# Strassen groups of a decoder layer: eviction bank by bank, two patterns, and loads at other places

## The chip, the core and the metric

The kernel runs on one core of a Trainium2 chip. A core has a matrix engine (TensorE, PE in the profile, with its weight loads as PEld), a vector engine (VectorE, DVE), a scalar engine (ScalarE, ACT), GpSimd (POOL), and a queue that issues most transfers (SyncE, SP). Each engine works through its own queue in order. Products land in PSUM, a memory of eight banks of 128 × 512 float32; everything else works in SBUF. The metric is the device time of one execution in microseconds (us), as the median of several runs.

## The reference

One layer on 256 tokens of width 2048: a SwiGLU block (FFN 1), a mixing block (sliding-window attention beside a gated linear recurrence), a second SwiGLU block (FFN 2), a gated embedding, and a final norm.

```python
def swiglu(h, w_gate, w_up, w_down):
    return (jax.nn.silu(h @ w_gate) * (h @ w_up)) @ w_down
...
        h = rmsnorm(x, ffn1_norm[l])
        x = x + 0.5 * swiglu(h, ffn1_w_gate[l], ffn1_w_up[l], ffn1_w_down[l])

        h = rmsnorm(x, mix_norm[l])
        proj = h @ w_in[l]
...
        x = x + merged @ w_out[l]

        h = rmsnorm(x, ffn2_norm[l])
        x = x + 0.5 * swiglu(h, ffn2_w_gate[l], ffn2_w_up[l], ffn2_w_down[l])

        g = jax.nn.sigmoid(rmsnorm(x, ple_norm[l]) @ ple_w_gate[l])
        x = x + g * (p[l].astype(x.dtype) @ ple_w_proj[l])
    return rmsnorm(x, final_norm)
```

The gate and up weights of an FFN are 2048 × 5632, the down weights 5632 × 2048, all float32.

## The kernel before

**Numbers in two parts.** Products are made from float32 values that are split into a high and a low part: ScalarE copies a weight block to `whi` (L117), VectorE subtracts it to get `wlo` (L118), and three products (high × high, high × low, low × high) are summed in PSUM. A weight block is 128 × 1024 floats, 512 KB, and is called an item below. `Weights` (L32 to L133) keeps the items' order: `load` issues the transfer of an item on SyncE (L92, eight buffers `raw`), `prep` makes its two parts (five buffers each for `whi` and `wlo`), `next` hands it out, prepares four items ahead (`AHEAD`) and calls `pump`. `pump` counts: a function given to `later(n, fn)` is called at the n-th pump from then, so n is a place in the order of items.

**The order of instructions.** The kernel is written with a scheduler in front: it puts the instructions of each engine in an order when the program is built, by readiness in its own estimate of time and by priority, which is the order of writing unless `high_priority(offset)` moves it ahead by that many instructions. Loads and splits of items after the twelfth have `PRIO`, 3000 (L87, L102). `keep_in_program_order` pins a transfer behind what was written before it on its queue (L533). At run time each engine keeps that order and waits at the head of its queue for what is not ready.

**The FFN.** `ffn` (L443) goes through the 11 chunks of 512 hidden columns in five slices (`FF_SLICES`): the chunks of a slice, then a share of the down products, four output blocks `nb` of 512 columns each (L488). A chunk's result `e` is transposed and split into `act` tiles by `to_act` (`transpose_split`, L327); those of a slice are queued behind its last chunk, the first two at once, the others at later pumps (L483 to L487). Chunk 0 of FFN 1 is computed plainly, while the activations' scale is still being made. The other 21 chunks go through `strassen_group` (L381).

**A Strassen group** computes gate and up of one chunk, for two halves of 128 tokens. The inner dimension is cut into four quarters `q`. `PATTERN` (L138) gives each a kind. A quarter "S" makes seven products of sums (roles 0 to 6: P1, P2, Q3, Q6, Q7, Q5, P4), one bank each, six matmuls each; its weights are four items and sums of them (L108 to L112, three at role 3, one at role 6). A quarter "P" makes the products plainly, four items of twelve matmuls: gate into the banks P2 and P4, up into Q3 and PE_. With "SPSP" P1, Q6, Q7 and Q5 are complete after the third quarter and the other four after the last. The banks are combined by nine instructions, one copy on ScalarE (L418) and eight additions on VectorE (`tt`, L402): p1, v2 and three more after the third quarter, in the order of writing (L415 to L422), and four at the end (L435 to L440), with SiLU in between (`silu`, L468, handed in as `last_first`). Then `e` = up × SiLU(gate) (L473, in FFN 2 L475 with a scale). None of these has a raised priority. All eight PSUM banks are used by a group: four from `acc`, four from `misc`, and transposes and down products take theirs from the same two.

**The activations of a group** are made by `scaled_parts` (L345): x, scaled and transposed, is split for a quarter "P" (`ap`, L251) or summed and split for a quarter "S" (`af` L365 and L369, `as` L373 and L374). In FFN 1 this needs the whole of x for the norm: `load_x` (L544) loads the eight pieces at pumps 4 to 7 (L551) and sums their squares (L255); `r_first` makes the scale; `scaled_parts` of quarter q comes at pump 9 + q (L643).

**Constants of the mixing block** are made by `mix_constants` (L572) at pump 60 (L638), which is the last item of chunk 2, the last of FFN 1's first slice: small loads on SyncE (L574, `hlb` among them), two loads of masks, and 44 short instructions on VectorE (L578 to L636) with some on ScalarE.

**The pumps of FFN 1**: chunk 0 has 16 items, every group 22, a slice's down products 16 (the last slice's 24). So pumps 279 to 300 are chunk 10, and 301 to 324 the last down products.

Of the kernel before, what the change touches and what calls it, by code (L numbers as in the profile page):

```python
# [10 lines left out]
F32 = mybir.dt.float32  # L11
# [7 lines left out]
P = 128  # L19
# [115 lines left out]


FF_SLICES = (((0, 3), (0, 2)), ((3, 5), (2, 4)), ((5, 7), (4, 6)), ((7, 9), (6, 8)), ((9, 11), (8, 11)))
PATTERN = "SPSP"  # L138
MIX = (
    ("i", 0), ("fq", 0), ("fq", 1), ("og", 0), ("kv", 0), ("fq", 2),  # L140
    ("q", 0), ("fq", 3), ("q", 1), ("i", 1), ("og", 1),
# [4 lines left out]
def weight_order():  # L146
    order = []

    def add(name, *idx):
        order.append((name, tuple(idx)))  # L150

    def block(name, nb, kg1=8, kg0=0):
        for kg in range(kg0, kg1):
            add(name, kg, nb)

    def ffn(n):
        for (a, b), (da, db) in FF_SLICES:
            for c in range(a, b):
                g, u = f"ffn{n}_gate", f"ffn{n}_up"
                if n == 1 and c == 0:  # L160
                    block(g, c)
                    block(u, c)
                    continue
                for q, kind in enumerate(PATTERN):
                    if kind == "S":
                        order.extend(("S", (g, c), (u, c), q, role) for role in range(7))
                    else:
                        order.extend((v, (2 * q + k, c)) for k in range(2) for v in (g, u))
            for nb in range(4):
                block(f"ffn{n}_down", nb, 2 * db, 2 * da)  # L170

    ffn(1)
    for what, j in MIX:
        if what == "fq":
            for h in (2 * j, 2 * j + 1):
                for w in ("w_f", "w_q"):
# [20 lines left out]
def decoder_layer(ctx: ExitStack, tc: tile.TileContext, io, out):  # L197
# [144 lines left out]
                nc.tensor.transpose(pt[:, c, t * P:(t + 1) * P], srcs[t][:, i * P:(i + 1) * P], ident)  # L342
        return pt

    def scaled_parts(A, q, s, gain):  # L345


        xs = [etile(name="xs") for _ in range(2)]
        for t in range(2):
            nc.scalar.activation(xs[t], x[t][q], AF.Copy, scale=s[:, t:t + 1])  # L350
        if PATTERN[q] == "P":
            A[q] = [atile(name="ap") for _ in range(2)]
            for kp in range(2):
                pt = transposed(xs, kp, "tx")
                for c in range(2):
                    f = 4 * q + 2 * kp + c
                    split_scaled(A[q][kp][:, c], pt[:, c], gain[:, f:f + 1])
            return
        full = [atile([P, 4, 2, P], F32, name="af") for _ in range(2)]
        quarter = full[0].rearrange("p (k c) t n -> p k c t n", k=2)  # L360
        for kp in range(2):
            pt = transposed(xs, kp, "tx")
            for c in range(2):
                f = 4 * q + 2 * kp + c
                nc.scalar.activation(quarter[:, kp, c], pt[:, c].rearrange("p (t n) -> p t n", t=2), AF.Copy, scale=gain[:, f:f + 1])  # L365
        a11, a21, a12, a22 = (quarter[:, k, :, t] for k in range(2) for t in range(2))
        a5, a6, a7, a3 = (full[1][:, i] for i in range(4))
        for o, u, v in ((a5, a21, a22), (a6, a11, a5), (a7, a21, a11), (a3, a12, a6)):
            nc.vector.tensor_tensor(o, u, v, op=ALU.subtract)  # L369
        parts = []  # L370
        for i in range(2):
            hi, lo = (atile([P, 4, 2, P], name="as") for _ in range(2))
            nc.scalar.copy(hi, full[i])  # L373
            nc.vector.tensor_tensor(lo, full[i], hi.bitcast(F32), op=ALU.subtract)  # L374
            parts.append((hi, lo))
        (rh, rl), (ch, cl) = parts
        raw = lambda k, t: lambda c: (rh[:, 2 * k + c, t], rl[:, 2 * k + c, t])
        mix = lambda i: lambda c: (ch[:, i, c], cl[:, i, c])
        A[q] = (raw(0, 0), raw(1, 0), mix(3), mix(1), mix(2), mix(0), raw(1, 1))

    def strassen_group(first, second, A, last_first):  # L381


        banks = {}
# [8 lines left out]
        for i in range(7):  # L393
            bank(i)

        def mm(i, stat, mov):
            todo = 6 * PATTERN.count("S") * (i < 7) + 12 * PATTERN.count("P") * (i in (P2, Q3, P4, PE_))
            done[i] = done.get(i, 0) + 1
            nc.tensor.matmul(bank(i), stat, mov, start=done[i] == 1, stop=done[i] == todo)  # L399

        def tt(out, a, b, op):
            nc.vector.tensor_tensor(out, a, b, op=op)  # L402

        g, u = (atile([P, 2, 512], F32, name="ff") for _ in range(2))
        for q, kind in enumerate(PATTERN):
            if kind == "S":
                for role in range(7):
                    hi, lo = (v.rearrange("p (c n) -> p c n", c=2) for v in W.next(("S", first, second, q, role)))
# [3 lines left out]
                        mm(role, sl, hi[:, c])  # L412
                    for c in range(2):
                        mm(role, A[q][role](c)[0], lo[:, c])
                if q == PATTERN.rindex("S"):  # L415
                    tmp = atile([P, 2, 512], F32, name="st")
                    p1, v2 = tmp[:, 0], tmp[:, 1]
                    nc.scalar.copy(p1, banks[P1])  # L418
                    tt(v2, banks[Q6], p1, ALU.subtract)
                    tt(g[:, 1], banks[Q7], v2, ALU.add)  # L420
                    tt(u[:, 0], banks[Q5], v2, ALU.add)
                    tt(u[:, 1], banks[Q5], g[:, 1], ALU.add)  # L422
            else:
                for k in range(2):
                    for (name, nb), (b0, b1) in ((first, (P2, P4)), (second, (Q3, PE_))):
# [6 lines left out]
                        for c in range(2):  # L432
                            for t, b in enumerate((b0, b1)):
                                mm(b, A[q][k][:, c, 0, t * P:(t + 1) * P], lo[:, c])
        tt(g[:, 0], banks[P2], p1, ALU.add)  # L435
        last_first(g, 0)
        tt(g[:, 1], banks[P4], g[:, 1], ALU.subtract)
        last_first(g, 1)
        tt(u[:, 0], banks[Q3], u[:, 0], ALU.add)
        tt(u[:, 1], banks[PE_], u[:, 1], ALU.add)  # L440
        return g, u

    def ffn(n, A, hT, r_of, on_block):  # L443
# [8 lines left out]
        for (a, b), (da, db) in FF_SLICES:  # L452
            for c in range(a, b):
# [13 lines left out]
                def silu(g, t):  # L467
                    nc.scalar.activation(g[:, t], g[:, t], AF.Silu, scale=1.0 if n == 1 else r_of()[:, t:t + 1])  # L468

                e, u = strassen_group((gate, c), (up, c), A, silu)  # L470
                for t in range(2):
                    if n == 1:
                        nc.vector.tensor_tensor(e[:, t], u[:, t], e[:, t], op=ALU.mult)  # L473
                    else:
                        nc.vector.scalar_tensor_tensor(e[:, t], u[:, t], r_of()[:, t:t + 1], e[:, t], op0=ALU.mult, op1=ALU.mult)  # L475
                es[c] = e
            late = []
            for c in range(da, b):
# [69 lines left out]
    load_in_order(ident, io["ident"])  # L548
    for nb in range(4):
        for t in range(2):  # L550
            W.later(4 + nb, lambda t=t, nb=nb: load_x(t, nb))  # L551
    first = []

    def r_first():
# [14 lines left out]
    omlb = const.tile([P, 8], F32, name="omlb")  # L569
    cs = const.tile([P, 2, 2, 16], F32, name="cs")  # L570

    def mix_constants():  # L572
        for t_, n_ in ((cpT, "cpT"), (sink, "sink"), (hlb, "hlb"), (pos, "pos"), (freq, "freq")):
            load_in_order(t_, io[n_])  # L574
        nc.gpsimd.memset(neg, -3.0e38)
        wide = atile([P, 512], I32, name="wide")
        load_in_order(wide, io["masks"][:, 0:512])
        nc.vector.tensor_copy(lmask.rearrange("p a s -> p (a s)"), wide)  # L578
        wide = atile([P, P], I32, name="wide")
        load_in_order(wide, io["masks"][:, 512:640])  # L580
        nc.vector.tensor_copy(pmask, wide)


        lmx = const.tile([P, 8], F32, name="lmx")
# [50 lines left out]
            nc.scalar.activation(cs[:, t, 1, 0:8], ang[:, t], AF.Sin)  # L635
            nc.vector.tensor_copy(cs[:, t, :, 8:16], cs[:, t, :, 0:8])  # L636

    W.later(60, mix_constants)  # L638

    mhT, on_block, mrs = next_stage("mx", gains["mix"])  # L640
    A1 = {}
    for q in range(4):
        W.later(9 + q, lambda q=q: scaled_parts(A1, q, r_first(), gains["ffn1"]))  # L643
    ffn(1, A1, hT, r_first, on_block)
    hT = mhT

# [242 lines left out]
    def on_block(nb):  # L889

        for t in range(2):
            square_sum(ss2[:, t, nb:nb + 1], x[t][nb])
        if nb == 2:
            s3 = const.tile([P, 2], F32, name="s3")
            v3 = const.tile([P, 2], F32, name="v3")
            nc.vector.tensor_reduce(v3, ss2[:, :, 0:3], axis=AX.X, op=ALU.add)
            nc.vector.tensor_scalar(v3, v3, 1.0 / 1536, EPS, op0=ALU.mult, op1=ALU.add)
            nc.gpsimd.tensor_tensor(s3, v3, nhalf[:, 0:2], op=ALU.pow)
            nc.vector.tensor_tensor(v3, v3, s3, op=ALU.mult)
            scale2.extend((s3, v3))  # L900
            for q in range(3):
                W.later(1 + 2 * q, lambda q=q: scaled_parts(A2, q, s3, gains["ffn2"]))
        if nb == 3:
            r = inv_rms(ss2, "f2")
            nc.vector.tensor_tensor(r, r, scale2[1], op=ALU.mult)
            left2.append(r)
            W.later(2, lambda: scaled_parts(A2, 3, scale2[0], gains["ffn2"]))

    for nb in range(4):
        for g in GATES[nb]:  # L910
# [158 lines left out]
```

## Time and profile before

| What | Value |
| --- | --- |
| Median of three runs | 2217.03 us (2215.2 to 2217.91) |
| The profiled execution's own time | 2218.1 us |
| Its span, first to last instruction | 2216.0 us |
| Mean granted TensorE clock | 0.995 |
| Moved by DMA | 418.97 MB, mean 189 GB/s |
| VectorE splits (L118) | 907 of 1219 ns |
| ScalarE high parts (L117) | 907 of 1051 ns |

Rows of groups read: line, engine, operation, what it writes and reads, shape, count; then busy time and the mean duration of one in ns; then the engine's idle time just before them and what ended it. Rows in order of time read: start and duration in us, engine, line, operation; in brackets the idle time before and what ended it. A row of waits reads: who waited, for whom, total us, how many times, the longest.

### The profile page before, as it was taken

The numbers are of one execution on the slowest core, as the hardware profiler recorded it, in microseconds if no ns is written. First come the engines' busy times: TensorE is split into PE (matmuls) and PEld (weight loads), VectorE is DVE, ScalarE is ACT, GpSimd is POOL, SyncE is SP. The second block draws the span as 40 slices with busy tenths as digits, with TensorE's granted clock in tenths as the row PEclk, the third lists the DMA queues.
The fourth block names the chain that finished last, engine by engine and source line by source line (L and its number), as shares of the span: only waits on it lengthen the run. The fifth ranks groups of instructions, "written<-read, shape, count | busy, mean of one in ns | idle before, by whom it ended". The sixth has DMA issues, their size and how long they took to land.

```text
span 2216.0 us, 27978 instructions
## 1 busy us (share of the span) xinstructions
PE 2182.4 (98%) x10400; PEld 1795.3 (81%) x10400; DVE 1666.3 (75%) x1954; ACT 1168.4 (53%) x1482; POOL 12.7 (1%) x26
## 2 busy tenths in 40 slices
PE   8999999999999999999999999999999999999998
PEld 7778888888888888877888888787888888888887
DVE  6987979789796566776455555898897979789654
ACT  7644645455455444556444445565554545545554
POOL 0000000000000000000000000000000000000000
PEclk9999999999999999999999999999999999999999
DMA  8455556646466554544666665456555556646662
GB/s 305 166 204 171 201 180 227 210 171 228 155 245 185 182 166 151 158 146 148 191 190 191 189 190 180 152 193 217 185 217 176 191 189 219 212 177 221 201 195 87
DMA packets 118072, 418.97 MB, mean 189 GB/s; under 512 B 13744, under 2 KB 14128, under 8 KB 117936
## 3 DMA queue, kind: packets, MB, share of 16 engines
q1 hardware_dynamic: 117072, 415.83, 56.1%
q8 instruction: 82, 1.34, 0.2%
q10 hardware_dynamic: 864, 1.35, 0.2%
q14 instruction: 54, 0.44, 0.1%
HBM read 415.03 MB, written 2.10 MB: 188 GB/s over the span
## 4 chain that ended last, share of the span: by engine, by line
PE 94%; DVE 3%; DMA 1%; ACT 1%; issue 1%; POOL 0%; SPq 0%; ACTq 0%; POOLq 0%; DVEq 0%
PE ps L399 38%; PE pa L290 16%; PE pa L291 16%; PE pa L296 16%; PE pb L311 3%; PE pb L313 1%; DVE wlo L118 1%; PE tp L333 1%; PE lv L808 1%; DMA raw<-in_ffn_gate 1%; ACT whi L117 1%; DVE raw L101 1%; DMA x<-in_x 0%; PE tx L506 0%; PE sc L726 0%
## 5 line engine op out<-in xcount | busy, mean ns | idle before, releaser
L118 DVE TENSOR_TENSOR wlo<-raw,whi 128x1024 fp32r<-128x1024 f32 (+1 forms) x907 | 1079.4, 1219 | 446.1 <-ACT whi L117 440.9
L117 ACT CAST whi<-raw 128x1024 fp32r<-128x1024 f32 (+1 forms) x907 | 930.5, 1051 | 888.6 <-PE pa L291 468.1
L399 PE MATMUL ps<-whi,ap 128*128 128x512 f32 x1344 | 337.2, 389 | 3.2 <-ACT whi L117 3.2
L399 PE MATMUL ps<-whi,as 128*128 128x512 f32 x1176 | 318.8, 393 | 4.3 <-DVE ff L464 2.1
L399 PEld LDWEIGHTS ps<-whi,ap 128*128 128x128 f32 x1344 | 251.6, 188 | 57.5 <-ACT whi L117 4.5
L291 PE MATMUL pa<-whi,act 128*128 128x512 f32 x704 | 275.2, 392 | 3.9 <-DVE act L335 3.9
L290 PE MATMUL pa<-whi,act 128*128 128x512 f32 x704 | 277.3, 395 | 0.6 <-ACT act L334 0.6
L399 PEld LDWEIGHTS ps<-whi,as 128*128 128x128 f32 x1176 | 220.9, 189 | 55.8 <-ACT whi L117 3.0
L101 DVE TENSOR_TENSOR raw<-raw,raw 128x1024 f32<-128x1024 f32 x168 | 205.4, 1223 | 4.2
L290 PE MATMUL pa<-whi,hTmx 128*128 128x512 f32 x480 | 192.1, 400 | 0.0
L296 PE MATMUL pa<-wlo,act 128*128 128x512 f32 x704 | 190.2, 392 | 0.0
L291 PE MATMUL pa<-whi,hTmx 128*128 128x512 f32 x480 | 187.4, 391 | 0.0
L399 PE MATMUL ps<-wlo,ap 128*128 128x512 f32 x672 | 183.5, 390 | 2.5 <-DVE wlo L118 2.5
L399 PE MATMUL ps<-wlo,as 128*128 128x512 f32 x588 | 182.9, 392 | 0.0
L291 PEld LDWEIGHTS pa<-whi,act 128*128 128x128 f32 x704 | 132.9, 189 | 31.3 <-DVE act L335 4.6
L290 PEld LDWEIGHTS pa<-whi,act 128*128 128x128 f32 x704 | 132.8, 189 | 27.6 <-ACT act L334 0.9
L296 PEld LDWEIGHTS pa<-wlo,act 128*128 128x128 f32 x704 | 132.1, 189 | 27.3
L399 PEld LDWEIGHTS ps<-wlo,ap 128*128 128x128 f32 x672 | 126.1, 188 | 29.9 <-DVE wlo L118 3.8
L399 PEld LDWEIGHTS ps<-wlo,as 128*128 128x128 f32 x588 | 110.5, 189 | 24.4 <-DVE wlo L118 1.7
L296 PE MATMUL pa<-wlo,hTmx 128*128 128x512 f32 x480 | 128.4, 389 | 0.0
L290 PEld LDWEIGHTS pa<-whi,hTmx 128*128 128x128 f32 x480 | 90.1, 188 | 21.4 <-issue 2.5
L296 PEld LDWEIGHTS pa<-wlo,hTmx 128*128 128x128 f32 x480 | 90.1, 188 | 18.9
(238 smaller groups left out, 1994.2 us busy)
## 6 DMA issues: line engine op xcount, KB each, us to landing
raw<-in_ffn_up SPq DMA_DIRECT2D x176, 512.0 KB, 5.1
raw<-in_ffn_down SPq DMA_DIRECT2D x176, 512.0 KB, 4.7
raw<-in_ffn_gate SPq DMA_DIRECT2D x175, 512.0 KB, 4.7
raw<-in_w_ga SPq DMA_DIRECT2D x32, 512.0 KB, 3.5
raw<-in_w_gb SPq DMA_DIRECT2D x32, 512.0 KB, 3.5
raw<-in_w_out SPq DMA_DIRECT2D x32, 512.0 KB, 3.5
raw<-in_ple_gate SPq DMA_DIRECT2D x32, 512.0 KB, 3.5
raw<-in_w_i SPq DMA_DIRECT2D x16, 512.0 KB, 3.5
```

The lines of the kernel that those rows point to most:

```text
L101: add = lambda out, a, b: nc.vector.tensor_tensor(out, a, b, op=ALU.add)
L117: nc.scalar.copy(hi[:, c], src[:, c])
L118: nc.vector.tensor_tensor(lo[:, c], src[:, c], hi[:, c].bitcast(F32), op=ALU.subtract)
L290: nc.tensor.matmul(ps[t], ks[:, 0, tok], hi[:, c], start=(j == 0 and c == 0), stop=False)
L291: nc.tensor.matmul(ps[t], ks[:, 1, tok], hi[:, c], start=False, stop=False)
L296: nc.tensor.matmul(ps[t], ks[:, 0, tok], lo[:, c], start=False, stop=(last and c == 1))
L311: nc.tensor.matmul(ps, hi[:, c], mov(c), start=(first and c == 0), stop=False)
L313: nc.tensor.matmul(ps[:, 0:S], lo[:, c], mov(c)[:, 0], start=False, stop=False)
L333: nc.tensor.transpose(pt[:, c, t * P:(t + 1) * P], srcs[t][:, i * P:(i + 1) * P], ident)
L399: nc.tensor.matmul(bank(i), stat, mov, start=done[i] == 1, stop=done[i] == todo)
L808: nc.tensor.matmul(ps[a * 64:a * 64 + 64, i], k[:, c], q[:, c], start=True, stop=True)
```

## The change

`PATTERN` becomes one pattern for each FFN, and `scaled_parts` takes the kind of its quarter as an argument.

```diff
-PATTERN = "SPSP"
+PATTERN = {1: "PSPS", 2: "SPSP"}
```

In `strassen_group` the nine steps are put in a list, each with the banks it needs; after each item's matmuls `evict` takes from the head of the list all steps whose banks are complete, with a priority 1000 ahead of that of the weight splits. The list's order depends on the last quarter's kind. The third tile (`tmp`, for p1 and v2) is taken from the same buffers as before, at the group's start.

```diff
+        def todo(i):
+            return 6 * pattern.count("S") * (i < 7) + 12 * pattern.count("P") * (i in (P2, Q3, P4, PE_))
+
         def mm(i, stat, mov):
...
+        def evict():
+
+            while steps and all(done.get(b) == todo(b) for b in steps[0][0]):
+                with tc.high_priority(offset=PRIO + 1000):
+                    steps.pop(0)[1]()
+
+        g, u, tmp = (atile([P, 2, 512], F32, name="ff") for _ in range(3))
+        p1, v2 = tmp[:, 0], tmp[:, 1]
+        steps = {
+            "p1": ((P1,), lambda: nc.scalar.copy(p1, banks[P1])),
+            "g0": ((P1, P2), lambda: (tt(g[:, 0], P2, p1), silu(g, 0))),
+            "v2": ((P1, Q6), lambda: tt(v2, Q6, p1, ALU.subtract)),
+            "v3": ((Q6, Q7), lambda: tt(g[:, 1], Q7, v2)),
+            "w": ((Q6, Q5), lambda: tt(u[:, 0], Q5, v2)),
+            "v4": ((Q7, Q5), lambda: tt(u[:, 1], Q5, g[:, 1])),
+            "g1": ((P4, Q5), lambda: (tt(g[:, 1], P4, g[:, 1], ALU.subtract), silu(g, 1))),
+            "u0": ((Q3, Q5), lambda: tt(u[:, 0], Q3, u[:, 0])),
+            "u1": ((PE_, Q5), lambda: tt(u[:, 1], PE_, u[:, 1])),
+        }
+        by_end = "p1 g0 v2 v3 w v4 u0 u1 g1" if pattern[-1] == "S" else "p1 v2 v3 w v4 g0 g1 u0 u1"
+        steps = [steps[k] for k in by_end.split()]
+        for q, kind in enumerate(pattern):
...
-                if q == PATTERN.rindex("S"):
-                    tmp = atile([P, 2, 512], F32, name="st")
-                    p1, v2 = tmp[:, 0], tmp[:, 1]
-                    nc.scalar.copy(p1, banks[P1])
-                    tt(v2, banks[Q6], p1, ALU.subtract)
-                    tt(g[:, 1], banks[Q7], v2, ALU.add)
-                    tt(u[:, 0], banks[Q5], v2, ALU.add)
-                    tt(u[:, 1], banks[Q5], g[:, 1], ALU.add)
+                    evict()
...
+                        evict()
-        tt(g[:, 0], banks[P2], p1, ALU.add)
-        last_first(g, 0)
-        tt(g[:, 1], banks[P4], g[:, 1], ALU.subtract)
-        last_first(g, 1)
-        tt(u[:, 0], banks[Q3], u[:, 0], ALU.add)
-        tt(u[:, 1], banks[PE_], u[:, 1], ALU.add)
+        assert not steps
```

The two products that make `e` (L473, L475) get the same priority:

```diff
+                with tc.high_priority(offset=PRIO + 1000):
+                    for t in range(2):
```

The loads of x and FFN 1's `scaled_parts` come two pumps earlier:

```diff
-            W.later(4 + nb, lambda t=t, nb=nb: load_x(t, nb))
+            W.later(2 + nb, lambda t=t, nb=nb: load_x(t, nb))
...
-        W.later(9 + q, lambda q=q: scaled_parts(A1, q, r_first(), gains["ffn1"]))
+        W.later(7 + q, lambda q=q: scaled_parts(A1, q, r_first(), gains["ffn1"], PATTERN[1][q]))
```

`mix_constants` is cut in two, the loads (the masks in one transfer, now of 640 columns) and the arithmetic, at two other places:

```diff
-    def mix_constants():
+    def load_mix_constants():
         for t_, n_ in ((cpT, "cpT"), (sink, "sink"), (hlb, "hlb"), (pos, "pos"), (freq, "freq")):
             load_in_order(t_, io[n_])
         nc.gpsimd.memset(neg, -3.0e38)
-        wide = atile([P, 512], I32, name="wide")
-        load_in_order(wide, io["masks"][:, 0:512])
-        nc.vector.tensor_copy(lmask.rearrange("p a s -> p (a s)"), wide)
-        wide = atile([P, P], I32, name="wide")
-        load_in_order(wide, io["masks"][:, 512:640])
-        nc.vector.tensor_copy(pmask, wide)
+        wides.append(atile([P, 640], I32, name="wide"))
+        load_in_order(wides[0], io["masks"])
+
+    def mix_constants():
+        nc.vector.tensor_copy(lmask.rearrange("p a s -> p (a s)"), wides[0][:, 0:512])
+        nc.vector.tensor_copy(pmask, wides[0][:, 512:640])
...
-    W.later(60, mix_constants)
+    W.later(290, load_mix_constants)
+    W.later(308, mix_constants)
```

More of the change, by code (lines that the diff above doesn't have):

```diff
@@ L163, in ffn @@
                     continue
-                for q, kind in enumerate(PATTERN):
+                for q, kind in enumerate(PATTERN[n]):
                     if kind == "S":
@@ L343, in transposed, with scaled_parts @@
         return pt
-    def scaled_parts(A, q, s, gain):
+    def scaled_parts(A, q, s, gain, kind):
         xs = [etile(name="xs") for _ in range(2)]
@@ L350, in scaled_parts @@
             nc.scalar.activation(xs[t], x[t][q], AF.Copy, scale=s[:, t:t + 1])
-        if PATTERN[q] == "P":
+        if kind == "P":
             A[q] = [atile(name="ap") for _ in range(2)]
@@ L379, in scaled_parts, with strassen_group @@
         A[q] = (raw(0, 0), raw(1, 0), mix(3), mix(1), mix(2), mix(0), raw(1, 1))
-    def strassen_group(first, second, A, last_first):
+    def strassen_group(first, second, A, pattern, silu):
         banks = {}
@@ L394, in strassen_group, with tt @@
             bank(i)
+        def todo(i):
+            return 6 * pattern.count("S") * (i < 7) + 12 * pattern.count("P") * (i in (P2, Q3, P4, PE_))
         def mm(i, stat, mov):
-            todo = 6 * PATTERN.count("S") * (i < 7) + 12 * PATTERN.count("P") * (i in (P2, Q3, P4, PE_))
             done[i] = done.get(i, 0) + 1
[L399 to L405, printed above, removed]
+            nc.tensor.matmul(bank(i), stat, mov, start=done[i] == 1, stop=done[i] == todo(i))
+        def tt(out, b, other, op=ALU.add):
+            nc.vector.tensor_tensor(out, banks[b], other, op=op)
+        def evict():
[18 more added lines that the diff above has]
+        for q, kind in enumerate(pattern):
             if kind == "S":
@@ L468, in silu @@
                     nc.scalar.activation(g[:, t], g[:, t], AF.Silu, scale=1.0 if n == 1 else r_of()[:, t:t + 1])
[L470 to L475, printed above, removed]
+                e, u = strassen_group((gate, c), (up, c), A, PATTERN[n], silu)
+                with tc.high_priority(offset=PRIO + 1000):
+                    for t in range(2):
+                        if n == 1:
+                            nc.vector.tensor_tensor(e[:, t], u[:, t], e[:, t], op=ALU.mult)
+                        else:
+                            nc.vector.scalar_tensor_tensor(e[:, t], u[:, t], r_of()[:, t:t + 1], e[:, t], op0=ALU.mult, op1=ALU.mult)
                 es[c] = e
@@ L570, in decoder_layer @@
     cs = const.tile([P, 2, 2, 16], F32, name="cs")
-    def mix_constants():
+    wides = []
+    def load_mix_constants():
         for t_, n_ in ((cpT, "cpT"), (sink, "sink"), (hlb, "hlb"), (pos, "pos"), (freq, "freq")):
@@ L901, in on_block @@
             for q in range(3):
-                W.later(1 + 2 * q, lambda q=q: scaled_parts(A2, q, s3, gains["ffn2"]))
+                W.later(1 + 2 * q, lambda q=q: scaled_parts(A2, q, s3, gains["ffn2"], PATTERN[2][q]))
         if nb == 3:
@@ L906, in on_block @@
             left2.append(r)
-            W.later(2, lambda: scaled_parts(A2, 3, scale2[0], gains["ffn2"]))
+            W.later(2, lambda: scaled_parts(A2, 3, scale2[0], gains["ffn2"], PATTERN[2][3]))
     for nb in range(4):
```

## The prediction

> **What bounds the kernel now.** First the summary at the head of the profile, then its chain that ended last.
>
> ```profile
> span 2216.0 us, 27978 instructions
> PE 2182.4 (98%) x10400; PEld 1795.3 (81%) x10400; DVE 1666.3 (75%) x1954; ACT 1168.4 (53%) x1482; POOL 12.7 (1%) x26
> PE 94%; DVE 3%; DMA 1%; ACT 1%; issue 1%; POOL 0%; SPq 0%; ACTq 0%; POOLq 0%; DVEq 0%
> ```
>
> TensorE is the bound, and this change takes no matmul away. So all it can win is the time in which TensorE stands or runs slowly. The next views say where that is not: the costliest group (its mean record is 389 ns), the chain in order of time, and the table of stretches (columns: length, PE, PEld, DVE, ACT, POOL, clock, DMA). The four stretches are one group of a middle slice, a middle slice's down products, and the first slice's two groups with what lies between.
>
> ```profile
> L399 PE MATMUL ps<-whi,ap 128*128 128x512 f32 x1344 | 337.2, 389 | 3.2 <-ACT whi L117 3.2
> 202.84 81.87 PE ps L399 x360
> 202.84:243.80 40.96, 40.96 (x182) 33.56 (x181) 38.81 (x38) 24.85 (x26) 0.00 (x0) 1.00 0.57 206
> 412.00:457.00 45.00, 45.00 (x208) 37.34 (x207) 30.05 (x32) 17.48 (x20) 0.00 (x0) 1.00 0.49 152
> 57.00:109.00 52.00, 48.09 (x206) 37.27 (x203) 49.06 (x52) 31.34 (x36) 0.00 (x0) 1.00 0.47 164
> 109.00:150.00 41.00, 38.98 (x167) 31.48 (x167) 36.60 (x39) 22.61 (x25) 0.00 (x0) 0.96 0.68 243
> ```
>
> Two middle groups are 360 matmuls without a break, 81.87/360 = 0.227 us apart. There the eviction order costs nothing today. But VectorE is busy 38.81 of 40.96 us, so a group has only 2.15 us to spare there; the down products have 15. What can be won lies in FFN 1's first slice. TensorE's waits between 57 and 118 us (columns: total, times, longest):
>
> ```profile
> PE ps L399 <- DVE ff L464: 2.1, 1, 2.1
> PE ps L399 <- DVE wlo L118: 1.2, 2, 0.6
> PE ps L399 <- ACT whi L117: 1.2, 3, 0.7
> PE ps L399 <- DVE ff L402: 1.0, 1, 1.0
> PE ps L399 <- DVE ap L251: 0.3, 1, 0.3
> ```
>
> Five rows, eight waits, 5.8 us. A matmul's record is 0.39 us long while the next can start after 0.227, so each wait loses 0.16 more than the idle time says: 5.8 + 8 × 0.16 = **7.1 us**. Next comes the turn from that slice's last group to its down products, TensorE first, then VectorE and the SyncE queue:
>
> ```profile
> 151.68 0.66 PE L333 MATMUL tp<-ident,ff 128*128 128x128 f32 x4 [0.97 <-DVE ff L402]
> 156.11 1.22 PE L291 MATMUL pa<-whi,act 128*128 128x512 f32 x2 [2.85 <-DVE act L335]
> 157.13 0.63 PE L290 MATMUL pa<-whi,act 128*128 128x512 f32 x1
> 157.56 0.63 PE L291 MATMUL pa<-whi,act 128*128 128x512 f32 x1
> 155.01 0.17 DVE L585 TENSOR_TENSOR lmx<-hlb 128x8 f32<-128x8 f32 x1 [2.19 <-DMA hlb<-in_hlb]
> 151.42 1.43 SPq L533 DMA_DIRECT2D hlb<-in_hlb  x1
> ```
>
> A constant's first instruction (L585) stands at the head of VectorE's queue, 2.19 us, until its load lands; the split that TensorE needs (L335) is queued behind it. TensorE loses 0.97 + 2.85 + 2 × 0.16 = 4.1 us. Afterwards matmuls are 0.43 us apart (157.13 to 157.56). The granted clock in three stretches, TensorE only, says why:
>
> ```profile
> 114.46:117.87 3.41, 3.41 (x9) 0.50 0.75 303
> 155.42:162.25 6.83, 6.14 (x14) 0.50 0.12 42
> 1401.28:1408.11 6.83, 5.65 (x14) 0.50 0.74 285
> ```
>
> At half clock a matmul costs 0.20 us more: 9 × 0.20 = 1.8 us, 14 × 0.20 = 2.8 us, and as much again at FFN 2's start.
>
> [...] Here it halved at 114.46 with no single idle of more than 1.0 us in the stretch before, so a bunch of short waits is enough. [...]
>
> **The change part by part.**
>
> *Mixing constants.* Their last VectorE instruction (the first is L585 above):
>
> ```profile
> 174.52 0.24 DVE L636 COPY cs<-cs 128x16 f32<-128x16 f32 x2
> ```
>
> Nothing is removed: five small loads, the 44 short VectorE instructions between these two rows (7.8 us in all, 0.1 to 0.4 each) and two table loads on ScalarE move from pump 60 to pumps 290 (loads) and 308 (arithmetic). The two mask loads become one: one issue fewer. The lost 4.1 + 2.8 = 6.9 us should go, but not all, since the turn itself remains. FFN 2 has the same turn without constants (TensorE's waits, 1515 to 1532 us):
>
> ```profile
> PE pa L291 <- DVE act L335: 1.1, 1, 1.1
> PE pa L290 <- ACT act L334: 0.6, 1, 0.6
> ```
>
> 1.7 + 2 × 0.16 = 2.0 us remain. With "PSPS" the last product to end is P4, and its SiLU and product come after it; I add 0.5. **Gain 4.4.** Bounds: 0 (the stall comes back whole) to 6.9. At their new place the instructions lie beside the last down products, where VectorE idles 15 of 45 us (412 to 457 above). Their users come after the 24 down blocks and eight "i" blocks, so nobody waits. If that cover were gone, they would cost their 7.8 us. The SyncE queue gets the loads during chunk 10; the raw loads behind them are late by about their issue times, at most some 3 us, against loads that run several blocks ahead.
>
> *x loaded two pumps earlier, scaled parts too, and "PSPS" in FFN 1.* VectorE's queue and the work that should move up (columns of the second: busy, mean ns, idle before):
>
> ```profile
> 32.51 1.23 DVE L118 TENSOR_TENSOR wlo<-raw,whi 128x1024 fp32r<-128x1024 f32 x1 [4.35 <-ACT whi L117]
> 35.17 1.23 DVE L118 TENSOR_TENSOR wlo<-raw,whi 128x1024 fp32r<-128x1024 f32 x1 [1.43 <-ACT whi L117]
> 39.34 1.23 DVE L118 TENSOR_TENSOR wlo<-raw,whi 128x1024 fp32r<-128x1024 f32 x1 [2.58 <-ACT whi L117]
> L374 DVE TENSOR_TENSOR as<-af,as 128x1024 fp32r<-128x1024 f32 x4 | 4.9, 1217 | 0.0
> L251 DVE SCALAR_TENSOR_TENSOR ap<-tx,vecs,ap 128x256 fp32r<-128x256 f32 x8 | 3.7, 477 | 0.2 <-ACT ap L250 0.2
> L369 DVE TENSOR_TENSOR af<-af,af 128x256 f32<-128x256 f32 x4 | 1.7, 419 | 0.0
> L369 DVE TENSOR_TENSOR af<-af 128x256 f32<-128x256 f32 x4 | 1.6, 418 | 0.0
> ```
>
> The parts are 4.9 + 3.7 + 1.7 + 1.6 = 11.9 us of VectorE, all after 36 us, and from there to 118 us VectorE is nearly full (49.06 of 52). Two pumps are two blocks of 12 matmuls, 2 × 12 × 0.227 = 5.4 us. Before the first parts VectorE idles (2.58 and 1.43 us among others), so of 5.4 us earlier some 3 to 4 find a place, and each us of work taken out of the full stretch gives TensorE at most one back. "PSPS" adds that the first group starts on a plain quarter: four blocks of 1.22 us on VectorE for 48 matmuls (10.9 us), where a Strassen quarter asks seven splits and four sums, 11 × 1.22 = 13.4 us, for 42 matmuls (9.5 us). That takes the pressure off 57 to 68 us, where half the idle time lies (2.07 us of it behind L464). Of 7.1 us I take 4.2, and the 1.8 us at half clock with them: **gain 6.0**, bounds 0 and 8.9.
>
> The price is on the SyncE queue and the DMA. Two more pairs of x loads pass in front of weight blocks 7 and 8.
>
> ```profile
> GB/s 305 166 204 171 201 180 227 210 171 228 155 245 185 182 166 151 158 146 148 191 190 191 189 190 180 152 193 217 185 217 176 191 189 219 212 177 221 201 195 87
> 23.24 1.06 ACT L117 CAST whi<-raw 128x1024 fp32r<-128x1024 f32 x1 [0.33 <-DMA raw<-in_ffn_gate]
> 28.25 0.39 PE L290 MATMUL pa<-whi,hTf 128*128 128x512 f32 x1
> ```
>
> Four loads of 128 × 512 × 4 bytes are 1.05 MB, 3.4 us at 305 GB/s. Block 7's high part is ready at 24.30 and first used at 28.25: 3.95 us of cover. So it is hidden by 0.5 us; I charge 0.3, bounds 0 and 3.4 (cover gone).
>
> *Evictions bank by bank, ahead of the splits.* The same nine instructions and two products a group, no more work. A group's eight VectorE evictions are 0.68 us each (rows below), 0.60 apart in a row ((1.88 − 0.68)/2); splits in a row are 1.13 apart. What changes is what waits: an eviction that is queued before its bank is finished holds every split behind it. Today:
>
> ```profile
> DVE ff L402 <- PE ps L399: 3.2, 10, 1.1
> L402 DVE TENSOR_TENSOR st<-ps,st x21: 679/680/683, 99.0 to 2029.9; 128x512 f32<-128x512 f32 x21
> 105.89 6.89 DVE L118 TENSOR_TENSOR wlo<-raw,whi 128x1024 fp32r<-128x1024 f32 x6
> 113.31 1.88 DVE L402 TENSOR_TENSOR ff<-ps,ff 128x512 f32<-128x512 f32 x3
> ```
>
> 21 groups, ten such waits, 3.2 us, hidden everywhere but in the first slice. Bounds for the middle groups: 0, since TensorE loses nothing there now and cannot gain, and the slower rival's 22 us. Nearest is the row of today; **I charge 0.6**.
>
> **Sum.** 4.4 + 6.0 − 0.3 − 0.6 = 9.5 us. The profiled execution took 2218.1 us (span 2216.0 and 2.1 around it), so 2208.6; it was 1.1 us above the median 2217.03, so **2207.5 us**.
>
> **The rivals.**
>
> *VectorE gives the start back.* If DVE stays full from 42 to 118 us, whatever order the parts have, the 6.0 us do not come: 2213.5. For it: 95% in every group. Against: idle time at 32 to 39 us.
>
> *The turn of FFN 1's groups.* A group now ends on a Strassen quarter and the next begins on a plain one, which writes P2 and, two matmuls later, P4. After Q5's last matmul come w, v4, u0, u1 and g1, 0.60 us apart: 3.0 us, of which the last role's six matmuls cover 1.36; the second bank is wanted 0.45 later. A wait of 1.2 us, or 2.3 with one split (1.13) between, at five turns: 9 us, 2216.5. For it: the one such wait of today, 1.0 us on L402. Against: if the plain quarter's matmuls on P2 and Q3 are issued first, 12 × 0.227 = 2.7 us cover it.
>
> [...]
>
> *Slower: evictions at the head of VectorE's queue.* If each of the eight evictions of a group waits w for its bank while splits stand behind it, a group loses 8w − 2.15 us as soon as w is over 0.27, and 21 groups eat the 9.5 us at w = 0.33. Today's ten waits average 0.32, the longest is 1.1. At w = 0.4: 21 × 1.05 = 22 us, 2229.5. Against: five slots of split weights and the down products' 15 us let VectorE catch up.
>
> *More than forecast.* The first slice loses all its waits (8.9 rather than 6.0) and the turn to the down products is clean in both FFNs (6.9 and 2.0): 17.8 us, less 0.9 charged: 2200.
>
> *The constants don't move as they should.* If their arithmetic is queued right behind the loads, DVE waits 2.19 us inside chunk 10. Half that cover is prefetch; it would cost 1 to 3 us, 2210.
>
> **How the numbers follow.** Forecast, with the constants' rival inside it: 0.50, its own range 2202 to 2212. More: 0.13. Start given back: 0.12. The turn of the groups: 0.10. Slower: 0.15. A measurement of this kernel tells apart about 0.2%, 4.4 us: faster is below 2212.6, slower above 2221.5. The forecast, the better case and a little of the third give faster 0.65; same 0.20; slower 0.15. The range runs from 2198 (the better case) to 2222 (w = 0.36), which leaves out most of the slower case and some of the best, under 2 in 10.
>
> **What would show it.** Right: TensorE's row at the first down products keeps a wait of 1 to 2 us and full clock; no wait on hlb; between 57 and 118 us under 3 us of idle; middle groups still 0.227 us a matmul. Wrong: TensorE waits for L402's successor or for wlo in every group of FFN 1, DVE idle on PE ps above 2 us a group, a half-clock stretch at a new place, or the first block of FFN 1 standing on a late weight load.

## The result, and the profile after

The changed kernel takes **2219.97 us** (median of 20 runs, 2218.39 to 2221.69), the kernel before 2217.12 us (median of 20, 2214.03 to 2219.24). The ratio is **1.0015, 95% interval 1.0008 to 1.0022**: a little slower, where 2207.5 us was forecast. The profiled execution took 2219.09 us, with a span of 2217.1, which is 1.1 us over the span before. It lies 0.9 us under its median and the one before 1.0 over its own, so the two profiles show only part of the 2.85 us between the medians. Most of the first 0.9 us goes with the clock: the profiled execution is one of four of the 20 with a mean clock of 0.997 (spans 2216.4 to 2217.2 us), the other 16 have 0.995 and a median span of 2217.9.

The same span hides large changes of both signs. The table is made from the traces: the start of the first matmul of each stage, and the differences between these starts.

| Stretch | before, us | after, us | difference |
| --- | --- | --- | --- |
| start to the first group | 57.29 | 57.52 | +0.23 |
| FFN 1's first slice: groups of chunks 1 and 2 | 94.80 | 83.33 | −11.47 |
| its down products (the first turn) | 50.59 | 54.00 | +3.41 |
| slices 2 to 4 and the groups of slice 5 | 464.26 | 464.48 | +0.22 |
| FFN 1's last down products | 69.24 | 71.33 | +2.09 |
| mixing block | 656.56 | 656.60 | +0.04 |
| FFN 2's first three groups | 133.37 | 134.51 | +1.14 |
| FFN 2, its first down products to its end | 580.25 | 585.83 | +5.58 |
| gated embedding and end | 109.64 | 109.55 | −0.09 |

So 11.5 us came in at the start, 5.5 went out in FFN 1's down products, and 6.7 in FFN 2. Two of these rows need care. With "PSPS" eight of the first slice's 24 transposes for `act` (0.109 us each) start behind the first down matmul instead of ahead of it, so 0.9 us of the −11.47 and of the +3.41 is only moved; in the later slices it is four of 16 (a pair of groups takes 82.35 us instead of 82.66, its down products 45.02 instead of 44.54). And FFN 2's first three groups had 3.4 us at half clock in this execution and 6.8 in the one before, so their +1.14 is too small by about 1 us (the first experiment shows that difference with the code of before).

First the head of the profile and its stretches (length, PE, PEld, DVE, ACT, POOL, clock, DMA): the first group with part of the second, the rest up to the first down matmul, and the stretches at half clock.

```profile
span 2217.1 us, 27937 instructions
PE 2180.3 (98%) x10400; PEld 1794.3 (81%) x10400; DVE 1669.1 (75%) x1954; ACT 1165.1 (53%) x1481; POOL 12.7 (1%) x26
...
57.00:109.00 52.00, 52.00 (x231) 43.03 (x231) 49.90 (x53) 29.91 (x34) 0.00 (x0) 1.00 0.48 171
109.00:140.85 31.85, 31.55 (x143) 25.51 (x141) 31.60 (x31) 21.16 (x24) 0.00 (x0) 1.00 0.58 209
147.40:154.20 6.80, 5.78 (x14) 4.52 (x15) 3.81 (x6) 1.04 (x1) 0.00 (x0) 0.50 0.62 216
```

TensorE is now busy for all 52 us where it was busy 48.09; VectorE is as full as it was. All the waits of the first slice's groups are gone, and its half-clock stretch too. Another half-clock stretch, 6.8 us, still comes with the first turn. VectorE's work in the whole stretch of these groups did fall, though (the kernel before, then the changed one, in the same columns):

```profile
57.29:152.09 94.80, 87.89 (x377) 69.39 (x376) 87.47 (x92) 55.56 (x61) 0.00 (x0) 0.98 0.57 202
57.52:140.85 83.33, 83.03 (x370) 68.14 (x368) 80.98 (x82) 50.55 (x57) 0.00 (x0) 1.00 0.52 186
```

Five splits of weights (L118, 46 before and 41 after) moved from it to the first turn (14 and 19), and five pieces of `ap` to the time ahead of it.

TensorE's five largest waits in the whole execution:

```profile
PE ps L401 <- ACT whi L117: 9.4, 7, 2.6
PE pa L291 <- DVE act L335: 7.0, 2, 5.5
PE pa L290 <- ACT whi L117: 6.2, 2, 5.1
PE pt L766 <- DVE s L760: 1.5, 2, 0.7
PE ps L401 <- DVE wlo L118: 1.3, 1, 1.3
```

Two rows have grown. The second was 3.9 us; its one wait of 5.5 us is the first turn. TensorE and VectorE there (start, duration, engine, line; idle before in brackets):

```profile
141.88 1.04 PE L333 MATMUL tp<-ident,ff 128*128 128x128 f32 x8
148.42 1.22 PE L291 MATMUL pa<-whi,act 128*128 128x512 f32 x2 [5.50 <-DVE act L335]
```

```profile
138.62 3.07 DVE L404 TENSOR_TENSOR ff<-ps,ff 128x512 f32<-128x512 f32 x5
141.61 0.68 DVE L485 TENSOR_TENSOR ff<-ff,ff 128x512 f32<-128x512 f32 x1
142.21 1.21 DVE L118 TENSOR_TENSOR wlo<-raw,whi 128x1024 fp32r<-128x1024 f32 x1
143.66 0.69 DVE L485 TENSOR_TENSOR ff<-ff,ff 128x512 f32<-128x512 f32 x1 [0.24 <-ACT ff L479]
144.27 3.49 DVE L118 TENSOR_TENSOR wlo<-raw,whi 128x1024 fp32r<-128x1024 f32 x3
147.68 2.48 DVE L335 TENSOR_TENSOR act<-tp,act 128x512 fp32r<-128x512 f32 x4
```

There is no wait for a constant any more. But TensorE wants L335, and VectorE first does evictions, two products and four splits of weights that TensorE will use only later. The products (L485) have the raised priority, the splits PRIO, and L335 none.

The first row of waits was 3.8 us in four waits. The new ones are in FFN 2 (TensorE, 1440 to 2040 us, then a middle pair of groups on VectorE and on TensorE):

```profile
PE ps L401 <- ACT whi L117: 6.8, 6, 1.9
```

```profile
1610.54 1.28 DVE L404 TENSOR_TENSOR ff<-ps,ff 128x512 f32<-128x512 f32 x2
1611.74 1.41 DVE L487 SCALAR_TENSOR_TENSOR ff<-ff,rstdf,ff 128x512 f32<-128x512 f32 x2
1613.06 3.49 DVE L118 TENSOR_TENSOR wlo<-raw,whi 128x1024 fp32r<-128x1024 f32 x3
1616.47 1.22 DVE L101 TENSOR_TENSOR raw<-raw,raw 128x1024 f32<-128x1024 f32 x1
```

```profile
1618.89 1.20 PE L401 MATMUL ps<-whi,as 128*128 128x512 f32 x4 [0.96 <-ACT whi L117]
```

Here the next group's first quarter is late: its last sum (L101 at 1616.47) stands behind two products of 0.74 us and three splits; ScalarE needs the sum for the high part, TensorE the high part.

### The profile page after: what moved, and what is told of

It is laid out like the page before. It is cut to its first block, busy times and chain, and to the rows that moved or that the text cites. A ratio compares the mean times of both kernels' runs of the same rounds, so it can differ in the third digit from the quotient of the medians.

```text
span 2217.1 us, 27937 instructions
## 1 busy us (share of the span) xinstructions
PE 2180.3 (98%) x10400; PEld 1794.3 (81%) x10400; DVE 1669.1 (75%) x1954; ACT 1165.1 (53%) x1481; POOL 12.7 (1%) x26
## 5 line engine op out<-in xcount | busy, mean ns | idle before, releaser
L118 DVE TENSOR_TENSOR wlo<-raw,whi 128x1024 fp32r<-128x1024 f32 (+1 forms) x907 | 1082.0, 1220 | 440.0 <-ACT whi L117 434.0
L101 DVE TENSOR_TENSOR raw<-raw,raw 128x1024 f32<-128x1024 f32 x168 | 205.7, 1224 | 5.2
L404 DVE TENSOR_TENSOR ff<-ps,ff 128x512 f32<-128x512 f32 x168 | 106.9, 681 | 4.9 <-PE ps L401 4.9
```

Of the source, the lines that this page charges most:

```text
L101: add = lambda out, a, b: nc.vector.tensor_tensor(out, a, b, op=ALU.add)
L118: nc.vector.tensor_tensor(lo[:, c], src[:, c], hi[:, c].bitcast(F32), op=ALU.subtract)
L404: nc.vector.tensor_tensor(out, banks[b], other, op=op)
```

## The experiments

The theory after the result: the earlier x and "PSPS" made the gain; the raised priority made both losses, because it puts work that nobody wants yet in front of what TensorE wants next. Rivals: the constants cost what they cost at any place; the order of the nine steps, or a group's end on a Strassen quarter, makes the losses by itself. Stages are read from the trace as in the table above, unless a time is given; a pair is the two groups of a slice. The first seven runs are one execution each. Stages that run at full clock mostly agree within 0.1 us between executions of the same code. But the start up to the first group took between 56.2 and 57.5 us in the traces, and a stage with a half-clock stretch varied by up to 2.4 us, so a difference of 2 or 3 us between two spans says nothing by itself.

**The constants alone.** The kernel before, with the constants as the change has them.

```diff
-    W.later(60, mix_constants)
+    W.later(290, load_mix_constants)
+    W.later(308, mix_constants)
```

> The kernel before with the mixing constants alone at pumps 290 and 308. If the constants made the stall of the first turn to the down products (6.9 us in the kernel before), the stretch from the first down matmul to the next group falls from 50.6 us to 46 or 47, and the last down products of FFN 1 keep 69.2 us: a profiled span near 2211. If the splits of weights queued ahead of the activations' split make it, the stretch stays within 1 us of 50.6. If the constants' arithmetic in the last down products costs what the changed kernel shows there (71.3 us), that stretch is 71 us here too.

Span 2209.1 us, 6.9 below before. The first turn takes 46.53 us (50.59 before), the groups ahead of it 93.35 (94.80), the last down products 69.48. TensorE's only wait from 143 to 165 us, and the clock there:

```profile
PE pa L291 <- DVE act L335: 1.1, 1, 1.1
```

```profile
148.00:156.00 8.00, 6.86 (x37) 5.38 (x36) 6.62 (x11) 4.48 (x7) 0.00 (x0) 1.00 0.48 139
```

The constants did make that stall and its half clock, and beside the last down products they cost 0.24 us. By themselves they do what the prediction said. (Of the 6.9 us about 1 is in FFN 2's first groups, 132.40 against 133.37, where the stretch at half clock was 3.4 us long instead of 6.8, and 0.7 in the start, 56.57 against 57.29.)

**x and the activations earlier, alone.** The kernel before, with two numbers changed.

```diff
-            W.later(4 + nb, lambda t=t, nb=nb: load_x(t, nb))
+            W.later(2 + nb, lambda t=t, nb=nb: load_x(t, nb))
...
-        W.later(9 + q, lambda q=q: scaled_parts(A1, q, r_first(), gains["ffn1"]))
+        W.later(7 + q, lambda q=q: scaled_parts(A1, q, r_first(), gains["ffn1"]))
```

> The kernel before with x and FFN 1's activations two pumps earlier, nothing else. The changed kernel takes 83.3 us from its first group to its first down matmul, the kernel before 94.8. If the earlier work on VectorE gave that, it is below 87 here; if the pattern PSPS gave it, it stays above 91. FFN 2 keeps its times (133.4 us for its first three groups, 82.7 us for each pair).

Span 2212.6. The groups take 90.58 us: 4.2 of the 11.5, between the two expectations. One wait is left there, and 6.8 us at half clock with it, where the kernel before had 3.4; the first turn grows by 1.5 us to 52.04:

```profile
PE ps L399 <- DVE ff L464: 2.9, 1, 2.9
```

**FFN 2 at normal priority.** The changed kernel; FFN 2's evictions and products not raised.

```diff
-                with tc.high_priority(offset=PRIO + 1000):
+                with tc.high_priority(offset=PRIO + 1000 if pattern[-1] == "S" else 0):
                     steps.pop(0)[1]()
...
-                with tc.high_priority(offset=PRIO + 1000):
+                with tc.high_priority(offset=PRIO + 1000 if n == 1 else 0):
                     for t in range(2):
```

> The changed kernel with the evictions and the products of FFN 2 at normal priority, those of FFN 1 raised as they are. If the raised priority makes FFN 2's loss, the pairs of groups fall from 83.9 to 82.7 us, the first three groups from 134.5 to 133.4, and the span from 2217 to about 2211. If the order of the nine steps makes it, the times stay at 83.9 and 2217.

Pairs of groups take 82.67 us, as before the change (83.94 after); the first three 133.21. Span 2210.1. The raised priority makes FFN 2's loss, and the order of the steps does not.

**Its products alone at normal priority**, its evictions still raised (the second half of the diff above).

> The changed kernel with the two products of FFN 2 (L487) at normal priority, its evictions still raised. A pair of groups loses 1.28 us in the changed kernel. If the two products (0.74 us each, ahead of the last sum of the next group's first quarter) make it, a pair takes 82.7 us here; if the evictions do, it stays at 83.9; if both, it lies between.

Pairs take 82.70 us, so **the two products make all of a pair's loss and the evictions none**. The first three groups take 133.77, between 133.21 and 134.51, with one more wait of 1.2 us than without raised evictions; there the evictions do cost some 0.6 us. Span 2209.4. The same place on VectorE, where the sum now comes first:

```profile
1609.08 3.49 DVE L118 TENSOR_TENSOR wlo<-raw,whi 128x1024 fp32r<-128x1024 f32 x3
1612.49 1.22 DVE L101 TENSOR_TENSOR raw<-raw,raw 128x1024 f32<-128x1024 f32 x1
1613.62 1.41 DVE L487 SCALAR_TENSOR_TENSOR ff<-ff,rstdf,ff 128x512 f32<-128x512 f32 x2
```

**The first turns raised.** The changed kernel; the transposes and splits that the first down products want are raised like the evictions.

```diff
                 if i < 2:
-                    fn()
+                    with tc.high_priority(offset=PRIO + 1000 if a == 0 else 0):
+                        fn()
```

> The changed kernel with the first two transposes and splits of activations in each FFN's first slice raised to the evictions' priority. The stretch from the first down matmul to the next group is 54.0 us in FFN 1 of the changed kernel, 5.5 us of it one wait for L335 behind four splits of weights. If the queue order is the cause, it falls to 46 or 47, with full clock, and the span from 2217 to about 2210; if the activations are late for another reason (SiLU, the last bank), it stays above 51.

The first turn takes 46.41 us (54.00 after), at full clock, FFN 2's 45.09 (46.81); span 2207.3. The activations could be ready; only the place in VectorE's queue was wrong:

```profile
141.57 0.68 DVE L335 TENSOR_TENSOR act<-tp,act 128x512 fp32r<-128x512 f32 x1
143.04 0.69 DVE L485 TENSOR_TENSOR ff<-ff,ff 128x512 f32<-128x512 f32 x1 [0.78 <-ACT ff L479]
143.65 0.68 DVE L335 TENSOR_TENSOR act<-tp,act 128x512 fp32r<-128x512 f32 x1
144.25 6.89 DVE L118 TENSOR_TENSOR wlo<-raw,whi 128x1024 fp32r<-128x1024 f32 x6
```

**SPSP in both.** The changed kernel with the old pattern in FFN 1.

```diff
-PATTERN = {1: "PSPS", 2: "SPSP"}
+PATTERN = {1: "SPSP", 2: "SPSP"}
```

> The changed kernel with SPSP in both FFNs, all else as it is. If PSPS gave the gain of the first slice, its groups take 88 us or more instead of 83.3; if the raised priority and the earlier x gave it, they stay under 85. If the loss at the turns is that of a group that ends on a Strassen quarter, FFN 1's first turn falls from 54.0 to 48 or less and its last down products from 71.3 to 69.5; and FFN 1's pairs then lose as FFN 2's do, 83.9 instead of 82.4.

Span 2219.9. The first slice's groups take 89.25 us, the first turn 46.73, the last down products 69.29, and FFN 1's pairs 83.80. So "PSPS" gives 5.9 us at the start, takes 7.3 back at the first turn (0.4 of both is four transposes that move) and 2.0 in the last down products, and spares FFN 1 the loss of the raised products. (The span is 2.8 us above the changed kernel's partly because FFN 2's first groups, the same code, had 10.2 us at half clock instead of 3.4.) The waits in the groups of the first slice, which "PSPS" has not:

```profile
PE ps L401 <- DVE ff L475: 2.9, 1, 2.9
PE ps L401 <- ACT whi L117: 1.1, 1, 1.1
```

**No raised priority at all**, "PSPS" kept (both offsets 0).

> The changed kernel with no raised priority for evictions or products, PSPS in FFN 1 kept. If the raised priority matters in FFN 1 at all, a group that ends on a Strassen quarter now waits for its banks at the turn of groups: FFN 1's pairs above 82.4 us, by up to 2.3. If it only displaces splits, FFN 1's pairs stay at 82.4 and its first turn falls from 54.0 to 50 or less. FFN 2's pairs take 82.7 in both.

Span 2209.8. FFN 1's pairs take 82.08 us, so at the turns of FFN 1's groups no bank is waited for even with unraised evictions. At the first turn to the down products one is: the transposes' bank comes from an eviction that is now queued behind nine splits of weights.

```profile
142.56 2.31 PE L333 MATMUL tp<-ident,ff 128*128 128x128 f32 x8 [3.87 <-DVE ff L404]
```

```profile
130.16 10.43 DVE L118 TENSOR_TENSOR wlo<-raw,whi 128x1024 fp32r<-128x1024 f32 x9
140.50 4.99 DVE L404 TENSOR_TENSOR ff<-ps,ff 128x512 f32<-128x512 f32 x8
```

The groups up to there, with this wait in them, take 88.11 us; FFN 1's pairs keep their times and its first down products are short (47.55), because the wait has come ahead of them. From 57 to 118 us TensorE has no wait in this kernel: "PSPS" with the earlier x empties that stretch without any raised eviction. The expectation for the first turn is met in its number alone: groups and turn together take 135.7 us here, 137.3 in the changed kernel and 129.8 with L335 raised. So the raised priority is at most 1.7 us of the first turn's loss. What makes the loss is that splits of weights go ahead of what the turn wants, of the eviction here and of L335 in the changed kernel. Whether "PSPS" would empty the first slice without the earlier x was not run.

**Three edits together**: FFN 2 at normal priority, the first turns raised, the constants at another place.

```diff
-    W.later(290, load_mix_constants)
-    W.later(308, mix_constants)
+    W.later(106, load_mix_constants)
+    W.later(124, mix_constants)
```

> The changed kernel with FFN 2's evictions and products at normal priority, the first slices' first two transposes and splits raised, and the constants beside the second slice's down products (pumps 106 and 124). If the three effects add up: span 2217.1 - 6.9 (FFN 2) - 7.6 (FFN 1's first turn) - 1.7 (FFN 2's) - 2.1 (last down products) = 2199, a ratio to the kernel before of 0.992. If the constants cost 2 us wherever they stand, the second slice's down products take 47 us instead of 45.0 and the span is 2201.

2205.49 us against 2218.26 of the kernel before, ratio **0.9937 (0.9923 to 0.995)**, span 2202.7. The second slice's down products take 47.03 us, for one wait:

```profile
284.72 0.73 PE L291 MATMUL pa<-whi,act 128*128 128x512 f32 x2 [1.69 <-DVE act L335]
```

and the last ones still 70.81. So moving the constants gained nothing: they cost 2.0 us at the new place (45.02 in the changed kernel), as the last part of the expectation had it, but leaving the old place gave only 0.5 (71.33 to 70.81). What the last down products lose in "PSPS" is mostly not the constants'.

**Products normal in both FFNs, all turns raised**: the constants as in the change, FFN 2's evictions normal, FFN 1's evictions alone raised.

```diff
-                with tc.high_priority(offset=PRIO + 1000):
+                with tc.high_priority(offset=0):
                     for t in range(2):
...
                 if i < 2:
-                    fn()
+                    with tc.high_priority(offset=PRIO + 1000):
+                        fn()
```

> The changed kernel with the constants where the change put them, FFN 2's evictions and the products of both FFNs at normal priority, and the first two transposes and splits of activations raised in every slice. If the constants' arithmetic alone makes the loss in FFN 1's last down products (71.3 us against 69.2), it stays above 71; if the late split of activations and weights after a group that ends on a Strassen quarter makes it, it is 70 or less. The first slice's groups stay at 83.3 us if the raised evictions carry that gain, and go back towards 88 if the raised products do. Span 2200 to 2203.

**2199.16 us against 2218.02, ratio 0.9919 (0.9905 to 0.9932)**, span 2197.3, below the expected 2200 to 2203; about 1 us of that is a shorter half-clock stretch at FFN 2's start. First slice 83.08, so it does not need the raised products; first turn 45.67, last down products 70.00. TensorE's waits in the whole execution; what is left of them in the two FFNs is at their starts:

```profile
PE pa L290 <- ACT whi L117: 6.4, 2, 5.1
PE ps L401 <- ACT whi L117: 2.6, 1, 2.6
PE pt L767 <- DVE s L761: 1.5, 2, 0.7
PE ps L401 <- DVE wlo L118: 1.3, 1, 1.3
PE tx L342 <- ACT xs L350: 0.6, 1, 0.6
PE pa L290 <- ACT act L334: 0.2, 1, 0.2
```

**The same with the constants beside the second slice's down products** (the diff of pumps 106 and 124 above).

> The same with the constants beside the second slice's down products. There the wait of 1.85 us for L335 made 47.0 us of 45.0; with the split raised the stretch is 45 to 45.5 and the span 1 to 2 us below that of the other run. If the constants cost 2 us at every place, it stays at 47.

2199.58 us, ratio 0.9919 (0.9906 to 0.9933), span 2197.2: the second slice's down products take 44.96, the last ones 69.84. The expected 1 to 2 us over the other run did not come: the two are the same. Once the split that TensorE wants is ahead in the queue, the place of the constants does not matter. About 0.44 us of the last down products' 0.6 to 0.8 us over the kernel before is then no loss: in this pattern four more transposes (0.109 us each) stand in that stretch and not in the groups ahead.

## Why the prediction was wrong

The forecast took 9.5 us off the span, and it grew by 1.1: a miss of 10.6 us. Two terms failed, the turn to the first down products (4.4 gained in the forecast, 3.4 lost in the run: 7.8 off) and the evictions (0.6 charged, 6.7 lost: 6.1 off). The last down products, put at nothing, lost 2.1, and the start gained 5.5 more than forecast. The start and the turn belong together, since work moved from the one to the other: of the 10.4 us forecast for both 8.1 came. Taken so, the evictions' term is the largest miss. The measured time lies inside the range of 2198 to 2222 us, but by luck: that end of the range stood for evictions that wait for their banks (w = 0.36), and this is not what happened.

**The start was under-sized.** The prediction said "Of 7.1 us I take 4.2, and the 1.8 us at half clock with them: gain 6.0". All 7.1 and 1.8 went, and with them the wait of 1.1 us for the transposes' bank, which had been counted with the constants: 10.0 of the 11.5 us measured. Another 0.9 are the transposes that moved to the turn, no gain; 0.6 stay open. The shares are not separate: the earlier x alone gives 4.2, x and the raised priority without "PSPS" 94.80 − 89.25 = 5.6, all three 11.5. The reason given, that each us taken from VectorE's full stretch gives at most one back, was too narrow. In the first 52 us VectorE is as busy as it was (49.90 against 49.06) and yet no wait is left. Its order has changed: "PSPS" asks first for the cheap splits of a plain quarter. So has its amount over the whole stretch (87.47 to 80.98 us). How much each counts was not separated.

**The first turn failed**: "With 'PSPS' the last product to end is P4, and its SiLU and product come after it; I add 0.5. Gain 4.4". The constants' stall did go, as the run with them alone shows (4.1 us there, and 1.5 in the groups ahead). But the row of FFN 2 was no measure for a group that ends on a Strassen quarter. That quarter and the raised evictions and products together leave VectorE behind: 19 splits of weights start in the first turn, 15 in the run with SPSP in both and 15 in the run without raised priority. And the splits themselves have priority over L335. The prediction looked at when the activations would be ready, and not at what stands ahead of L335 in VectorE's queue. Measured: 3.4 us lost (0.9 of them the moved transposes), outside the bounds of 0 to 6.9 us of gain, and the half clock again. Raising L335 gave 7.6 us back.

**The last down products**: "At their new place the instructions lie beside the last down products, where VectorE idles 15 of 45 us". True for the constants alone (0.24 us). With "PSPS" the stage begins with the same backlog on VectorE (one split of weights at 661.65 us and five from 663.39 stand ahead of L335 at 669.07), and it lost 2.1 us: 0.44 are the moved transposes, and two waits are there that the kernel before has not (TensorE, 655 to 735 us). The wait for L503 is not there when the constants stand elsewhere (three edits); neither is there when L335 is raised in every slice and the products are not.

```profile
PE tx L518 <- DVE x L503: 0.6, 1, 0.6
PE pa L296 <- DVE wlo L118: 0.5, 1, 0.5
```

**The evictions were charged 0.6 and FFN 2 lost 6.7.** The bounds for the middle groups were right, 0 to 22; the choice within them was wrong. The slower rival had place and sign but not the mechanism. It expected evictions to wait for their banks at the head of the queue; those waits are few after the change too:

```profile
DVE ff L404 <- PE ps L401: 4.9, 10, 0.7
```

What costs is not an eviction that waits but a product that runs: the change raised the two products L487 along with the evictions, nothing needs them at that moment, and in a stage where VectorE has some 1.8 us to spare in a group (79.07 us busy of a pair's 82.66 before the change) they push the sum that gates the next items. The prediction noted the raised products as "no more work" and did not ask what they would stand in front of.

**What held.** The earlier x loads stay cheap. That 0.23 us stand beside the 0.3 forecast is no proof of the price: the same start took 56.2 to 57.5 us in the traces with the earlier loads, 56.6 and 57.3 in the two without. No wait for P4's bank at the turns of FFN 1's groups: with raised and with unraised evictions its pairs take 82.4 and 82.1 us, so the rival of the turn of the groups falls. The constants are not queued ahead of their loads' landing at the new place.

**The clock.** At half clock TensorE ran after 5.5 us of waiting at 148.42, and no longer at 114.46, where four short waits went. That the 1.8 us would go with the short waits was the author's reading of the trace: in the 3.41 us ahead of 114.46 TensorE was still busy for 1.78. In the changed kernel they went with them: the clock is 1.00 from 57 to 140.85 us.

What stays open: why the start gained 0.6 us more than its waits, and what the executions that were not profiled did in the 1.7 us between the medians that the two profiles don't show, beyond the clock.

## What to carry to other kernels

When an instruction is moved ahead on an engine that is nearly full, ask what it pushes back, and raise only what somebody waits for: here the evictions could be raised almost without harm (0.6 us in FFN 2's first groups), the two products behind them could not, and the split that TensorE did wait for had been left without any priority. A stall that is removed shows what is queued behind it; before its whole length is counted as gain, read what else stands in front of the waiting engine's operand. And a busy share says how full a queue is, not whether its order is right: the first slice lost all its waits with VectorE just as full, after some of its work had been put elsewhere and the rest in another order.

## What the runs showed of the hardware

From the first group to the end of FFN 2, TensorE ran at half clock in the kernel before for 3.41 us from 114.46 and for 6.83 us from 155.42 and from 1401.28; in the changed kernel for 6.83 us from 147.37 and for 3.42 us from 1396.65. How long it had been busy just before does not tell by itself whether the clock halved: in the kernel before it was busy for 1.78 us both in the 3.41 us from 63.26 and in the 3.41 us from 111.05, and half clock followed the second alone. The busy time is the profile's, whose matmul ends are modelled.

Waits of one length were not followed by the same clock either. TensorE waited 2.87 us for the product of chunk 0 in the run with x alone, until 67.23, and in the run with SPSP in both, until 67.01 (length, PE, clock, DMA; first three rows x alone, then two of SPSP in both):

```profile
62.92:66.33 3.41, 1.44 (x6) 1.00 1.01 377
66.33:69.74 3.41, 2.51 (x6) 0.50 0.74 303
69.74:73.16 3.42, 3.42 (x9) 0.50 0.18 30
64.31:67.72 3.41, 0.71 (x3) 1.00 0.95 335
67.72:71.14 3.42, 3.42 (x10) 0.50 0.44 180
```

In the first run the clock halved at 66.33, 0.90 us before the wait ended; in the 3.41 us from there TensorE was busy for only 2.51, and the next 3.42 us were at half clock too. In the other it halved at 67.72, 0.71 us after the wait had ended, and TensorE was busy for all of the 3.42 us from there. In the kernel before, 2.07 us at the same place were followed by no half clock. Why the clock halved where it did was not shown. By an estimate from the 14 matmuls that the 6.83 us from 155.42 held (14 × 0.20 us), a wait of 2 to 3 us was followed by a further loss of between nothing and about 3 us, which is part of why two kernels' stages should be compared stage by stage.
